# Softmax times V over 96 heads on one core: loads four heads ahead on SyncE, stores on the GpSimd queue, the cast of v on VectorE

## The chip, the cores and the metric

The kernel runs on one core of one Trainium2 chip. A core has a matrix engine (TensorE, in the profile PE, with its weight loads as PEld), VectorE (DVE), ScalarE (ACT), GpSimd (POOL) and SyncE (SP), which only waits and issues transfers here. All transfers between the device memory (HBM) and the on-chip buffer run on the core's 16 DMA engines. The metric is the device time of one launch in microseconds (us); lower is better. The time quoted is the median of several runs. A profile is of one single execution.

## The reference

Scores of 8 x 12 = 96 heads are given, 1024 x 1024 float32 for each head, and v, 1024 x 64 float32 for each head. The result is the softmax of the scores times v:

```python
batch, n_heads, seq, head_dim = 8, 12, 1024, 64
scores_max = np.max(scores, axis=-1, keepdims=True)
attn = np.exp(scores - scores_max)
attn = attn / (np.sum(attn, axis=-1, keepdims=True) + 1e-8)
return np.matmul(attn, v).astype(np.float32)
```

For each head 4 MB of scores and 256 KB of v come in, and 256 KB of result go out.

## The kernel before, in words

The loop runs over the 96 heads (`BH`), and in each head over `R` = 8 blocks of 128 query rows. One load brings the v of a head into `v_sb` (L100), and one load its scores into `s_nat` (L104): partition p holds query rows 8p to 8p+7, so each partition reads 32 KB that lie together. Only the last head loads its scores in four pieces of two blocks.

The work on a head goes through four engines. GpSimd casts v from float32 to fp16 into one of three buffers `vones` (L107), whose 65th column is a constant 1.0, so that the matrix product gives the row sums beside the result. ScalarE takes the exponential of two blocks at a time, `s_nat` to `p_nat` in fp16 (L113, four per head; no maximum is subtracted). TensorE transposes each block in eight 128 x 128 pieces into PSUM, `psT` (L117), VectorE copies them back, `pt` (L123), and TensorE multiplies them with `vones` into `psO`, eight matmuls that accumulate (L76). In the source the product of a block comes two blocks later than its transposes (`LAG` = 2, the list `pending` and the function `finish`). After each four blocks VectorE takes the reciprocal of the sums (L87) and multiplies (L88) into `out_sb`. When a head's eight blocks are done, one store writes `out_sb` back (L95).

Loads and stores are all issued by SyncE, one after the other: an instruction that has to wait there holds up every one behind it. SyncE issues the store of a head when VectorE has finished that head's `out_sb`. There are four buffers each for `s_nat` and `v_sb`, three for `out_sb`, six for `p_nat`, five for `pt`, five for `psT` and three for `psO`. A framework works out the semaphores and the order in which each engine gets its instructions; that order, and not only the order of the source lines, says which load stands behind which store.

Of the kernel before, what the change touches and what calls it, by code (L numbers as in the profile page):

```python
# [1 line left out]

# [5 lines left out]

FP32 = mybir.dt.float32
FP16 = mybir.dt.float16  # L10
EXP = mybir.ActivationFunctionType.Exp


@with_exitstack
def kernel(
    ctx: ExitStack,
    tc: tile.TileContext,
    scores: bass.AP,
    v: bass.AP,
    out: bass.AP,  # L20
):
    nc = tc.nc
    P = 128

    B, H, SQ, SK = scores.shape
    Bv, Hv, SKv, D = v.shape
    assert (B, H, SK) == (Bv, Hv, SKv)
    BH = B * H
    assert SQ % P == 0 and SK % P == 0
    R = SQ // P  # L30
    C = SK // P
    M = D + 1
    EB = 2
    G = 4
    LAG = 2
    NV = 3

    sc_bh = scores.rearrange("b h (p r) j -> (b h) p r j", p=P)  # L40
    v_bh = v.rearrange("b h (p c) d -> (b h) p c d", p=P)
    out_bh = out.rearrange("b h (p r) d -> (b h) p r d", p=P)

    const_pool = ctx.enter_context(tc.tile_pool(name="const", bufs=1))
    s_pool = ctx.enter_context(tc.tile_pool(name="spool", bufs=4))
    p_pool = ctx.enter_context(tc.tile_pool(name="ppool", bufs=6))
    v_pool = ctx.enter_context(tc.tile_pool(name="vpool", bufs=4))
    pt_pool = ctx.enter_context(tc.tile_pool(name="ptpool", bufs=5))
    ob_pool = ctx.enter_context(tc.tile_pool(name="obpool", bufs=3))
    rc_pool = ctx.enter_context(tc.tile_pool(name="rcpool", bufs=4))  # L50
    psT_pool = ctx.enter_context(tc.tile_pool(name="psTp", bufs=5, space=bass.MemoryType.PSUM))
    psO_pool = ctx.enter_context(tc.tile_pool(name="psOp", bufs=3, space=bass.MemoryType.PSUM))

    ident32 = const_pool.tile([P, P], FP32, name="ident32")
    make_identity(nc, ident32)
    ident16 = const_pool.tile([P, P], FP16, name="ident16")
    nc.vector.tensor_copy(out=ident16[:], in_=ident32[:])  # L57


    vones_bufs = []  # L60
    for k in range(NV):
        vo = const_pool.tile([P, C, M], FP16, name=f"vones{k}")
        nc.vector.memset(vo[:, :, D : D + 1], 1.0)  # L63
        vones_bufs.append(vo)

    pending = []

    def finish(u):

        n, r, pt, st = u  # L70
        g = r % G
        if g == 0:
            st["psO"] = psO_pool.tile([P, G, M], FP32, tag="psO", name="psO")
        psO = st["psO"]
        for c in range(C):
            nc.tensor.matmul(  # L76
                out=psO[:, g, :],
                lhsT=pt[:, c * P : (c + 1) * P],
                rhs=st["vones"][:, c, :],
                start=(c == 0),  # L80
                stop=(c == C - 1),
            )
        if g == G - 1:
            if r == G - 1:
                st["out_sb"] = ob_pool.tile([P, R, D], FP32, tag="out_sb", name="out_sb")
            recip = rc_pool.tile([P, G, 1], FP32, tag="recip", name="recip")
            nc.vector.reciprocal(out=recip[:], in_=psO[:, :, D : D + 1])  # L87
            nc.vector.tensor_tensor(  # L88
                out=st["out_sb"][:, r - G + 1 : r + 1, :],
                in0=psO[:, :, 0:D],  # L90
                in1=recip[:].to_broadcast([P, G, D]),
                op=mybir.AluOpType.mult,
            )
        if r == R - 1:
            nc.sync.dma_start(out=out_bh[n], in_=st["out_sb"][:])  # L95

    for n in range(BH):
        last = n == BH - 1
        v_sb = v_pool.tile([P, C, D], FP32, tag="v_sb", name="v_sb")
        nc.sync.dma_start(out=v_sb[:], in_=v_bh[n])  # L100
        s_nat = s_pool.tile([P, R, SK], FP32, tag="s_nat", name="s_nat")
        step = EB if last else R
        for r in range(0, R, step):
            nc.sync.dma_start(out=s_nat[:, r : r + step, :], in_=sc_bh[n, :, r : r + step, :])  # L104

        vones = vones_bufs[n % NV]
        nc.gpsimd.tensor_copy(out=vones[:, :, 0:D], in_=v_sb[:])  # L107
        st = dict(vones=vones)

        for r in range(R):  # L110
            if r % EB == 0:
                p_nat = p_pool.tile([P, EB, SK], FP16, tag="p_nat", name="p_nat")
                nc.scalar.activation(out=p_nat[:], in_=s_nat[:, r : r + EB, :], func=EXP)  # L113
            p_row = p_nat[:, r % EB, :].rearrange("p (q c) -> p c q", c=C)
            psT = psT_pool.tile([P, SK], FP16, tag="psT", name="psT")
            for c in range(C):
                nc.tensor.transpose(  # L117
                    out=psT[:, c * P : (c + 1) * P],
                    in_=p_row[:, c, :],
                    identity=ident16[:],  # L120
                )
            pt = pt_pool.tile([P, SK], FP16, tag="pt", name="pt")
            nc.vector.tensor_copy(out=pt[:], in_=psT[:])  # L123
            pending.append((n, r, pt, st))
            if len(pending) > LAG:
                finish(pending.pop(0))
    while pending:
        finish(pending.pop(0))


# [1 line left out]
_INS = ['scores', 'v']  # L132
_OUTS = [((8, 12, 1024, 64), 'float32')]


# [23 lines left out]
```

## Time and profile before

| What | Value |
|---|---|
| median of 3 runs | 1283.77 us (1282.96 to 1286.11) |
| the profiled execution | 1278.68 us, its span from first to last instruction 1276.9 us |
| PE, PEld busy | 797.7 us (62%), 760.6 us (60%) |
| ACT busy | 703.9 us (55%) |
| DVE busy | 619.7 us (49%) |
| POOL busy | 60.1 us (5%) |
| HBM read, written | 427.82 MB, 25.17 MB |
| mean granted TensorE clock | 0.764 of full speed |

Busy time is the time in which an engine executes something; issuing a transfer and waiting do not count. "L95" is line 95 of the kernel. In a list of groups, "<-" gives what was written and from what, then shapes, the count, the busy time, the mean duration of one in nanoseconds, and the time that the engine was idle just before, with what ended that idle time. The DMA lines give in tenths how busy the 16 DMA engines were in each of 40 equal slices, and the rate in each. The chain is the work that ended last, followed back from the end, each step to the thing that released it. SPq and POOLq are the instruction queues of SyncE and GpSimd.

### The profile page before, as it was taken

How to read it: one execution, taken by the hardware profiler on the slowest of the kernel's cores; microseconds unless marked ns; L12 is line 12 of the kernel's file. 1: busy time of each engine (PE TensorE's matmuls, PEld its weight loads, DVE VectorE, ACT ScalarE, POOL GpSimd, SP SyncE). 2: the span in 40 equal slices, each digit the busy share in tenths (PEclk: the TensorE clock that was granted, in tenths of full speed). 3: DMA queues.
4: the chain of work that ended last, by engine and by line, in shares of the span. 5: the costliest groups of instructions: out<-in, count | busy, mean ns of one | idle time of the engine just before them, and what ended most of it. 6: DMA issues, size and time to landing. Idle time of an engine off the chain costs nothing.

```text
span 1276.9 us, 27588 instructions
## 1 busy us (share of the span) xinstructions
PE 797.7 (62%) x12288; PEld 760.6 (60%) x12288; DVE 619.7 (49%) x1156; ACT 703.9 (55%) x385; POOL 60.1 (5%) x102
## 2 busy tenths in 40 slices
PE   4666576665656657566665656666575655656656
PEld 4566565665656556556655656656565655656556
DVE  3445454454555445445454544545454544545545
ACT  4464564655646455554645556465565645556465
POOL 0000000000000000000000000000000000000000
PEclk9777778777787777777777787778777777777778
DMA  9888988988979889898999889899888989879886
GB/s 402 327 358 365 356 363 347 377 351 358 377 316 368 365 358 378 329 370 348 360 377 365 362 345 375 334 364 377 361 363 328 366 363 376 362 312 374 356 346 264
DMA packets 42023, 454.76 MB, mean 356 GB/s; under 512 B 4656, under 2 KB 4656, under 8 KB 29232
## 3 DMA queue, kind: packets, MB, share of 16 engines
q1 hardware_dynamic: 41904, 453.00, 87.9%
q8 instruction: 96, 1.57, 0.5%
q14 instruction: 23, 0.19, 0.0%
HBM read 427.82 MB, written 25.17 MB: 355 GB/s over the span
## 4 chain that ended last, share of the span: by engine, by line
DMA 51%; PE 23%; DVE 8%; ACT 8%; issue 6%; SPq 4%; ACTq 0%
DMA s_nat<-in_scores_dram 51%; PE psT L117 17%; ACT p_nat L113 8%; PE psO L76 6%; DVE pt L123 4%; DVE out_sb L88 3%; SPq L100 2%; DVE recip L87 1%; SPq L95 1%; ACTq L113 0%; SPq L104 0%
## 5 line engine op out<-in xcount | busy, mean ns | idle before, releaser
L113 ACT ACTIVATE p_nat<-s_nat 128x2048 f16<-128x2048 f32 x384 | 702.6, 1900 | 564.7 <-DMA s_nat<-in_scores_dram 553.3
L117 PE MATMUL psT<-ident,p_nat 128*128 128x128 f16 x6144 | 634.9, 269 | 435.3 <-ACT p_nat L113 435.2
L123 DVE COPY pt<-psT 128x1024 f16<-128x1024 f16 x768 | 529.1, 690 | 599.5 <-PE psT L117 587.3
L117 PEld LDWEIGHTS <-p_nat 128*128 128x128 f16 x6144 | 538.5, 156 | 460.2 <-ACT p_nat L113 450.5
L76 PE MATMUL psO<-vones,pt 128*128 128x65 f16 x6144 | 345.6, 205 | 40.0 <-DVE pt L123 40.0
L76 PEld LDWEIGHTS <-pt 128*128 128x128 f16 x6144 | 298.4, 107 | 52.2 <-DVE pt L123 52.2
L107 POOL CAST vones<-v_sb 128x512 f16<-128x512 f32 x96 | 59.4, 619 | 1196.0 <-DMA v_sb<-in_v_dram 1094.1
L88 DVE TENSOR_TENSOR out_sb<-psO,recip 128x256 f32<-128x256 f32 x192 | 80.6, 420 | 3.3
L87 DVE RECIPROCAL recip<-psO 128x4 f32<-128x4 f32 x192 | 34.1, 178 | 50.0 <-PE psO L76 50.0
L113 ACT ACT_TABLE_LOAD x1 | 1.3, 1283 | 0.7 <-PEq L143 0.7
L63 DVE MEMSET vones<- 128x8 f16 x3 | 0.1, 65 | 0.8 <-PEq L143 0.8
L57 DVE CAST ident<-ident 128x128 f16<-128x128 f32 x1 | 0.2, 226 | 0.4 <-POOL ident masks.py:199 0.4
masks.py:199 POOL TENSOR_SCALAR_AFFINE_SELECT ident<-ident 128x128 f32<-128x128 f32 x1 | 0.3, 294 | 0.1
masks.py:197 POOL MEMSET ident<- 128x128 f32 x1 | 0.2, 205 | 0.3 <-POOLq L143 0.3
L143 POOL MEMSET const-float32-0.0<- 128x1 f32 x1 | 0.1, 99 | 0.2 <-issue 0.2
L143 POOL MEMSET const-bfloat16-1.0<- 128x1 bf16 x1 | 0.1, 102 | 0.0
L143 POOL MEMSET const-uint8-127<- 128x1 uint8 x1 | 0.1, 102 | 0.0
L143 POOL MEMSET const-float32-1.0<- 128x1 f32 x1 | 0.1, 99 | 0.0
## 6 DMA issues: line engine op xcount, KB each, us to landing
s_nat<-in_scores_dram SPq DMA_DIRECT2D x95, 4096.0 KB, 13.8
v_sb<-in_v_dram SPq DMA_DIRECT2D x96, 256.0 KB, 3.1
out_dram<-out_sb SPq DMA_DIRECT2D x96, 256.0 KB, 2.4
s_nat<-in_scores_dram SPq DMA_DIRECT2D x4, 1024.0 KB, 8.9
```

What stands on the lines that cost most here:

```text
L57: nc.vector.tensor_copy(out=ident16[:], in_=ident32[:])
L63: nc.vector.memset(vo[:, :, D : D + 1], 1.0)
L76: nc.tensor.matmul(out=psO[:, g, :], lhsT=pt[:, c * P : (c + 1) * P], rhs=st["vones"][:, c, :], start=(c == 0), stop=(c == C - 1),)
L87: nc.vector.reciprocal(out=recip[:], in_=psO[:, :, D : D + 1])
L88: nc.vector.tensor_tensor(out=st["out_sb"][:, r - G + 1 : r + 1, :], in0=psO[:, :, 0:D], in1=recip[:].to_broadcast([P, G, D]), op=mybir.Al ...
L95: nc.sync.dma_start(out=out_bh[n], in_=st["out_sb"][:])
L100: nc.sync.dma_start(out=v_sb[:], in_=v_bh[n])
L107: nc.gpsimd.tensor_copy(out=vones[:, :, 0:D], in_=v_sb[:])
L113: nc.scalar.activation(out=p_nat[:], in_=s_nat[:, r : r + EB, :], func=EXP)
L117: nc.tensor.transpose(out=psT[:, c * P : (c + 1) * P], in_=p_row[:, c, :], identity=ident16[:],)
L123: nc.vector.tensor_copy(out=pt[:], in_=psT[:])
L143: nc = _bacc.Bacc("TRN2", target_bir_lowering=False, num_devices=1)
```

## The change

Four things change. The loads are issued by a function `load`: four heads (`AHEAD` = 4) ahead of the loop, and then the load of head n + 4 at the last block of head n, after that head's exponentials. Each load is made to follow the load before it in SyncE's queue (`queue`, an order without a semaphore). The stores go out on GpSimd's queue. The cast of v is done by VectorE. The buffers stay as many as before (`AHEAD` is 4, as the counts were).

```diff
+    AHEAD = 4
...
-    s_pool = ctx.enter_context(tc.tile_pool(name="spool", bufs=4))
+    s_pool = ctx.enter_context(tc.tile_pool(name="spool", bufs=AHEAD))
...
-    v_pool = ctx.enter_context(tc.tile_pool(name="vpool", bufs=4))
+    v_pool = ctx.enter_context(tc.tile_pool(name="vpool", bufs=AHEAD))
...
         if r == R - 1:
-            nc.sync.dma_start(out=out_bh[n], in_=st["out_sb"][:])
+            nc.gpsimd.dma_start(out=out_bh[n], in_=st["out_sb"][:])
+
+    queued = []
+
+    def queue(dma):
+
+        if queued:
+            tc.add_manual_dep(
+                dma.ins,
+                queued[-1].ins.name,
+                mybir.DependencyInfo(mybir.DependencyClass.NoSync, mybir.DependencyReason.DATA),
+                reason="queue order",
+            )
+        queued.append(dma)
+
+    loaded = {}
+
+    def load(n):
+        v_sb = v_pool.tile([P, C, D], FP32, tag="v_sb", name="v_sb")
+        queue(nc.sync.dma_start(out=v_sb[:], in_=v_bh[n]))
+        s_nat = s_pool.tile([P, R, SK], FP32, tag="s_nat", name="s_nat")
+        step = EB if n == BH - 1 else R
+        for r in range(0, R, step):
+            queue(
+                nc.sync.dma_start(out=s_nat[:, r : r + step, :], in_=sc_bh[n, :, r : r + step, :])
+            )
+        loaded[n] = (s_nat, v_sb)
+
+    for n in range(min(AHEAD, BH)):
+        load(n)

     for n in range(BH):
-        last = n == BH - 1
-        v_sb = v_pool.tile([P, C, D], FP32, tag="v_sb", name="v_sb")
-        nc.sync.dma_start(out=v_sb[:], in_=v_bh[n])
-        s_nat = s_pool.tile([P, R, SK], FP32, tag="s_nat", name="s_nat")
-        step = EB if last else R
-        for r in range(0, R, step):
-            nc.sync.dma_start(out=s_nat[:, r : r + step, :], in_=sc_bh[n, :, r : r + step, :])
-
+        s_nat, v_sb = loaded.pop(n)
         vones = vones_bufs[n % NV]
-        nc.gpsimd.tensor_copy(out=vones[:, :, 0:D], in_=v_sb[:])
+        nc.vector.tensor_copy(out=vones[:, :, 0:D], in_=v_sb[:])
...
             nc.vector.tensor_copy(out=pt[:], in_=psT[:])
+            if r == R - 1 and n + AHEAD < BH:
+                load(n + AHEAD)
             pending.append((n, r, pt, st))
```

SyncE at the start of the program, before. The names carry numbers that count up with the heads: `s_nat_97`, `_252`, `_427`, `_602`, `_777` are the scores of heads 0 to 4, and `out_sb_205`, `_380`, `_555` the results of heads 0, 1 and 2.

```order
L100 DMA v_sb_95<-in_v_dram 128x512
L104 DMA s_nat_97<-in_scores_dram 128x8192
L100 DMA v_sb_250<-in_v_dram 128x512
L104 DMA s_nat_252<-in_scores_dram 128x8192
L100 DMA v_sb_425<-in_v_dram 128x512
L104 DMA s_nat_427<-in_scores_dram 128x8192
L95 DMA out_0_dram<-out_sb_205 128x512
L95 DMA out_0_dram<-out_sb_380 128x512
L100 DMA v_sb_600<-in_v_dram 128x512
L104 DMA s_nat_602<-in_scores_dram 128x8192
L95 DMA out_0_dram<-out_sb_555 128x512
L100 DMA v_sb_775<-in_v_dram 128x512
```

From then on the load of head n + 2 stands behind the store of head n. The same place on SyncE in the changed kernel (`s_nat_97`, `_101`, `_105`, `_109`, `_256`, `_431` are heads 0 to 5), with the semaphores on which a row waits:

```order
L115 DMA v_sb_95<-in_v_dram 128x512
L120 DMA s_nat_97<-in_scores_dram 128x8192
L115 DMA v_sb_99<-in_v_dram 128x512
L120 DMA s_nat_101<-in_scores_dram 128x8192
L115 DMA v_sb_103<-in_v_dram 128x512
L120 DMA s_nat_105<-in_scores_dram 128x8192
L115 DMA v_sb_107<-in_v_dram 128x512
L120 DMA s_nat_109<-in_scores_dram 128x8192
L115 DMA v_sb_254<-in_v_dram 128x512 [waits DMAHW0_49,DVE_49]
L120 DMA s_nat_256<-in_scores_dram 128x8192 [waits DMAHW1_49,Activation_49]
L115 DMA v_sb_429<-in_v_dram 128x512 [waits DMAHW2_49,DVE_49]
L120 DMA s_nat_431<-in_scores_dram 128x8192 [waits DMAHW3_49,Activation_49]
```

The stores have left SyncE, four heads are loaded before anything waits, and from head 4 on the load of v waits for the cast four heads earlier (on VectorE) and the load of the scores for the exponentials four heads earlier (on ScalarE).

VectorE around the change from head 0 to head 1, before (`out_sb_205` is head 0's result, `pt_266` and `pt_285` the first two blocks of head 1):

```order
L123 COPY pt_240<-psT_231 128x1024
L87 RECIPROCAL recip_295<-psO_222 128x4
L88 TENSOR_TENSOR out_sb_205<-psO_222,recip_295 128x256
L123 COPY pt_266<-psT_257 128x1024
L123 COPY pt_285<-psT_276 128x1024
```

And in the changed kernel (`out_sb_217` is head 0's result, `pt_278` and `pt_297` the first two blocks of head 1, `vones2_93<-v_sb_103` the cast of head 2's v):

```order
L146 COPY pt_252<-psT_243 128x1024
L88 RECIPROCAL recip_307<-psO_234 128x4
L89 TENSOR_TENSOR out_sb_217<-psO_234,recip_307 128x256
L130 CAST vones2_93<-v_sb_103 128x8x64
L146 COPY pt_278<-psT_269 128x1024
L146 COPY pt_297<-psT_288 128x1024
```

Between the last multiplication of a head and the first copy of the next there is now one cast, and it is the cast for the head after that one: the copies of head 1 stand behind the cast of head 2's v, those of head 2 behind the cast of head 3's, and so on. GpSimd is left with the 96 stores, each of which waits for VectorE, and from the ninth on for the landing of the store eight before it.

## The prediction

> **What bounds the kernel now.** First the page: how long, and which engine is full.
>
> ```profile
> span 1276.9 us, 27588 instructions
> PE 797.7 (62%) x12288; PEld 760.6 (60%) x12288; DVE 619.7 (49%) x1156; ACT 703.9 (55%) x385; POOL 60.1 (5%) x102
> ...
> DMA packets 42023, 454.76 MB, mean 356 GB/s; under 512 B 4656, under 2 KB 4656, under 8 KB 29232
> ...
> q1 hardware_dynamic: 41904, 453.00, 87.9%
> q8 instruction: 96, 1.57, 0.5%
> ```
>
> No compute engine is busy for two thirds of the span. The DMA engines are at 87.9 + 0.5 = 88.4%, so they are near their limit but not at it: 11.6%, or 148 us, they stand still. The chain and the waits say why.
>
> ```profile
> DMA s_nat<-in_scores_dram 51%; PE psT L117 17%; ACT p_nat L113 8%; PE psO L76 6%; DVE pt L123 4%; DVE out_sb L88 3%; SPq L100 2%; DVE recip L87 1%; SPq L95 1%; ACTq L113 0%; SPq L104 0%
> ```
> ```profile
> SPq L95 <- DVE out_sb L88: 1110.7, 96, 21.5
> ```
> ```profile
> ACT p_nat L113 <- DMA s_nat<-in_scores_dram: 553.3, 92, 11.6
> ```
>
> The chain alternates: half of it is the load of scores, the rest the head's way through ACT, PE and DVE, and back to SyncE. SyncE waits 1110.7 us at the stores (L95) for VectorE, and the next load stands behind each store. ACT in turn waits 553.3 us for loads. The timeline of SyncE shows one turn of the circle:
>
> ```profile
> 605.40 0.34 SPq L95 DMA_DIRECT2D out_dram<-out_sb  x1
> 605.84 0.38 SPq L100 DMA_DIRECT2D v_sb<-in_v_dram  x1
> 606.31 0.40 SPq L104 DMA_DIRECT2D s_nat<-in_scores_dram  x1
> 616.61 0.34 SPq L95 DMA_DIRECT2D out_dram<-out_sb  x1
> 617.04 1.07 SPq L100 DMA_DIRECT2D v_sb<-in_v_dram  x1
> 618.21 0.38 SPq L104 DMA_DIRECT2D s_nat<-in_scores_dram  x1
> 632.03 0.34 SPq L95 DMA_DIRECT2D out_dram<-out_sb  x1
> 632.47 0.38 SPq L100 DMA_DIRECT2D v_sb<-in_v_dram  x1
> 632.94 0.41 SPq L104 DMA_DIRECT2D s_nat<-in_scores_dram  x1
> ```
>
> The scores issued at 606.31 come back as a store at 632.03, and the load of the head after next leaves at 632.94: 26.63 us for two heads, 13.3 each, and 96 x 13.3 = 1278, the span. So the bound is a circle of load and compute with two heads in it, closed by SyncE's order. The windows show what it costs the DMA engines (columns: stretch, its length, busy time of each engine, granted clock, DMA share, GB/s):
>
> ```profile
> core 0: us, PE busy (x) PEld busy (x) DVE busy (x) ACT busy (x) POOL busy (x), PEclk, DMA share, GB/s
> 13.60:24.00 10.40, 8.04 (x122) 7.80 (x123) 5.86 (x10) 7.32 (x5) 0.62 (x1) 1.00 1.02 436
> 606.30:618.20 11.90, 7.86 (x128) 7.49 (x128) 6.46 (x12) 6.69 (x4) 0.62 (x1) 0.82 1.00 400
> 618.20:632.90 14.70, 8.86 (x128) 8.49 (x128) 6.46 (x12) 9.02 (x5) 0.62 (x1) 0.68 0.79 321
> ```
>
> Fed without a gap they move 400 to 436 GB/s; where the next load is late, 321.
>
> **The change, part by part.** *Stores leave SyncE and the loads run four heads ahead.* This opens the circle. The load of head n + 4 now waits for ACT's last exponential of head n, 7.32 us after that head has landed (the window's four), and there are then the heads n + 1 to n + 3 still queued. The queue should never run dry, and the DMA engines set the pace. Their price is the bytes, 454.76 MB, over the rate of a full queue, and for that I have rows from both sides:
>
> ```profile
> DMA packets 574, 8.88 MB, mean 423 GB/s; under 512 B 62, under 2 KB 62, under 8 KB 319
> ...
> q1 hardware_dynamic: 574, 8.88, 99.0%
> ```
>
> This is the stretch from 3 to 24 us, where three heads were queued at once: loads alone, 423 GB/s, 1075 us for all bytes. The best stretch (436) gives 1043 us; 606.3 to 618.2, with stores and v among the scores and a share of 1.00, gives 1137 at 400 GB/s; the packets of today laid end to end, 88.4% of the span, give 1129. I take the middle of 423 and 400, 411.5 GB/s: **1105 us**, since the new stream has stores in it, as the second row has, but no starts from an empty queue, as the first. Ahead of it lies the start, 2.0 us:
>
> ```profile
> 0.00:2.00 2.00, 0.00 (x0) 0.00 (x0) 0.36 (x4) 1.27 (x1) 0.70 (x6) 1.00 0.19 13
> 2.00:4.00 2.00, 0.00 (x0) 0.00 (x0) 0.00 (x0) 0.01 (x1) 0.40 (x1) 1.00 1.07 380
> ```
>
> Behind it lies the way of the last two blocks, priced from groups and from the chain in order of time:
>
> ```profile
> 620.08 1.92 ACT p_nat L113
> ...
> 625.36 0.85 PE psT L117 x8
> 626.21 0.44 PE psO L76 x8
> ```
> ```profile
> L123 DVE COPY pt<-psT 128x1024 f16<-128x1024 f16 x768 | 529.1, 690 | 599.5 <-PE psT L117 587.3
> ...
> L107 POOL CAST vones<-v_sb 128x512 f16<-128x512 f32 x96 | 59.4, 619 | 1196.0 <-DMA v_sb<-in_v_dram 1094.1
> L88 DVE TENSOR_TENSOR out_sb<-psO,recip 128x256 f32<-128x256 f32 x192 | 80.6, 420 | 3.3
> L87 DVE RECIPROCAL recip<-psO 128x4 f32<-128x4 f32 x192 | 34.1, 178 | 50.0 <-PE psO L76 50.0
> ...
> L57 DVE CAST ident<-ident 128x128 f16<-128x128 f32 x1 | 0.2, 226 | 0.4 <-POOL ident masks.py:199 0.4
> ...
> out_dram<-out_sb SPq DMA_DIRECT2D x96, 256.0 KB, 2.4
> ```
>
> An exponential 1.92, two blocks on PE 2 x 1.29, a copy 0.69, a last product 0.44, reciprocal and multiply 0.60, the store to landing 2.4: 8.6 us, and I say 9 with the issue. The sum is 2 + 1105 + 9 = 1116 us of span.
>
> *What is late next.* A head would then come every 11.5 us. ACT needs 7.32 of it. DVE has 6.46 and one cast more. PE in the slow rows above (clock 0.68 in that window) takes 0.85 + 0.44 = 1.29 us a block, 10.3 a head, and less when the clock is up (8.04 busy at 1.00 in 13.6 to 24). All stay under 11.5, PE by the least.
>
> *The cast goes from GpSimd to VectorE.* GpSimd's is 59.4 us in all (L107 above), idle 1196.0 us before it, so nothing is gained by its going. On VectorE the trace has no cast of 128x512 float32; the same operation on a quarter of it takes 226 ns (L57), the copy of twice the elements 690 (L123). I take 0.5 us, between 0.23 and 0.9 (four times 226); 48 us in all, to 668 busy. VectorE's idle time hides it, 587.3 us before the copies alone; without that cover it would cost its 48. As the order shows, the cast for head n + 1 stands ahead of the copies of head n, so all copies of head n, PE's products and the p_nat buffers behind them wait until v of head n + 1 is there. It is queued right behind the scores of head n, 256 KB, 0.6 us at 423 GB/s, while the first copy of head n needs an exponential (1.92) and eight transposes first. As long as the queue is full the wait is covered, and I cost it at nothing.
>
> *The store on GpSimd.* Its issue cost there is not in the trace. The nearest rows are SyncE's own issues (shortest, median and longest in ns):
>
> ```profile
> L100 SPq DMA_DIRECT2D v_sb<-in_v_dram x96: 327/384/1556, 0.7 to 1251.7; - x96
> ```
>
> They take 0.33 to 1.56 us, and GpSimd has nothing else left to do, so I take nothing. A store may be late by two heads (three `out_sb` buffers) before VectorE's multiply waits for it. That the store shares the DMA engines from another queue is the open point, next.
>
> **The rivals.** *A: a switch between queues costs.* In the old kernel loads and stores are on one queue, q1. What a foreign packet costs there is seen in q8: 96 packets of 16.4 KB hold 0.5% of 16 x 1276.9 us, 1.06 us each, where q1's 39.6 ns a KB (87.9% for 453.00 MB) would give 0.65. A foreign packet is thus some 0.4 us dearer, 0.3 to 0.5 by the rounding. A store has 8 packets on each of 16 engines (29232 - 4656 = 24576 of 2 KB, over 192 transfers of v and result). If each of them cost 0.41 more, a head would take 3.3 us more and the kernel 1116 + 315 = 1431 us: slower. One such cost per store gives +39, 1155; three, +118, 1234. It decides from four per store on: (1277 - 1116) / 96 = 1.7 us a head. Against it: q8's packets come from another source, singly, and the engines may hold both queues ready. By the Trainium skill ("DMA: Bandwidth & Descriptors", Queues, rings and completion order) a DMA engine takes the queues in turn and empties a whole packet of some 9 to 17 descriptors before it goes to the next; by that rule a store would be one switch and the sum 1155. No row here shows how a store is cut.
>
> *B: the long-run rate is capped.* The middle of the run moves 356 GB/s on the whole page, and the longest stretch above 400 that I have is the first 32 us (402 in the first slice):
>
> ```profile
> GB/s 402 327 358 365 356 363 347 377 351 358 377 316 368 365 358 378 329 370 348 360 377 365 362 345 375 334 364 377 361 363 328 366 363 376 362 312 374 356 346 264
> ```
>
> If memory gave no more than the 356 to 358 of the middle over a long time, the span would be 454.76 MB / 357 = 1274 + 11 = 1285, no change. Against it: a share of 0.79 stands beside the 321, and 400 comes with 1.00, at 606 us as at 13; the low mean goes with idle engines. By the Trainium skill (the same page, Specifications) the memory's limit for a core is about 358 GB/s, which would be this case; the 423 and 436 above speak against it for one core alone.
>
> *C: the change does not do what it says.* A load could still wait for the late part of the circle. By the order it waits for ACT and the cast only; then ACT would end up with the old 553.3 us of waits and the time at 1278.
>
> **How the numbers follow.** The profiled execution is 1278.68 us, 1.8 above its span, and the median 1283.77 is 1.004 of it. (1116 + 1.8) x 1.004 = **1122 us**. Chances: forecast, from 436 to 400 GB/s, 1060 to 1155: 0.64. A mild (two or three switch costs, 1155 to 1240): 0.17. A hard (slower, 1285 to 1435): 0.12. B: 0.05, C: 0.02, both about no change. The range takes in forecast and mild A, and leaves out the hard A, B and C; the low end is cut to 1070, 432 GB/s, since stores are in the stream: 1070 to 1240. Faster by over 0.3%, about what a measurement of this kernel can tell from no change: 0.64 + 0.17 = 0.81; within it 0.06 (B, C, less a part); slower 0.13.
>
> **What would show it.** Right: DMA share 97% or more in every slice, 400 to 425 GB/s, the chain nearly all loads of scores, SyncE's waits on ACT instead of DVE, ACT waiting about 4 us a head, and VectorE's casts near 0.5 us with no wait of length. The store of a head may land late, 10 us and more. Wrong: a share near 100% with a rate under 380 GB/s is A or B; A if packets of the scores got longer where stores run beside them, B if they are longer all the time. Gaps in the DMA row mean C, or that copies wait behind a cast. PE waiting for nothing means compute became the bound.

## The result, and the profile after

The changed kernel takes 1094.79 us (median of 4 runs, 1094.51 to 1095.15) against 1283.69 us before. The ratio is 0.8526, with a 95% interval of 0.8511 to 0.8541: 14.7% less time. 1122 us was forecast, 1070 to 1240 the range. The profiled execution took 1095.15 us, its span 1093.4 us.

The page of the changed kernel, in the parts that were shown of before:

```profile
span 1093.4 us, 27493 instructions
...
PE 784.1 (72%) x12288; PEld 745.6 (68%) x12288; DVE 656.1 (60%) x1252; ACT 704.0 (64%) x385; POOL 55.4 (5%) x102
...
DMA  9999999999999999999999999999999999999982
GB/s 394 428 430 426 429 427 425 424 426 431 425 432 423 423 429 426 426 429 428 429 421 430 425 424 433 422 432 425 424 427 421 435 423 424 428 425 428 428 363 93
...
q1 hardware_dynamic: 28080, 427.83, 92.0%
q0 software_dynamic: 7680, 25.17, 5.7%
q8 instruction: 96, 1.57, 0.6%
...
L96 POOL DMA_DIRECT2D out_dram<-out_sb x96 | 54.7, 570 | 1028.7 <-DVE out_sb L89 1028.7
...
L130 DVE CAST vones<-v_sb 128x512 f16<-128x512 f32 x96 | 41.1, 428 | 47.1 <-DMA v_sb<-in_v_dram 46.4
...
s_nat<-in_scores_dram SPq DMA_DIRECT2D x95, 4096.0 KB, 36.8
v_sb<-in_v_dram SPq DMA_DIRECT2D x96, 256.0 KB, 37.3
out_dram<-out_sb POOLq DMA_DIRECT2D x96, 256.0 KB, 10.7
```

The DMA row is full from the first slice to the last but two, and no slice in between is under 421 GB/s. The busy time of TensorE and ScalarE is nearly what it was; they do the same work in a shorter span. VectorE has the casts in addition, and what GpSimd has left is the issue of the stores. q0 is GpSimd's queue, and holds the stores. A load now takes 37 us from issue to landing, since three others stand before it.

SyncE's waits in the changed kernel, longest first (us in total, times, longest):

```profile
SPq L120 <- ACT p_nat L136: 680.7, 92, 7.4
SPq L120 <- DMA s_nat<-in_scores_dram: 276.8, 93, 8.4
SPq L179 <- DMA out_dram<-out_sb: 42.8, 2, 37.5
SPq L115 <- DVE pt L146: 14.4, 41, 0.5
SPq L179 <- PEq L179: 6.2, 2, 5.7
```

The 1110.7 us at the stores are gone. SyncE now waits for ScalarE, or for the older load whose semaphore it uses again, and with a full queue neither costs anything. What the span holds besides the full stream is at its end. The windows of the changed kernel, the middle first, then 3 us each:

```profile
4.00:1040.00 1036.00, 750.16 (x11728) 713.46 (x11729) 625.81 (x1191) 673.58 (x368) 51.91 (x91) 0.81 1.01 427
```
```profile
1052.00:1055.00 3.00, 1.07 (x26) 0.82 (x23) 2.04 (x6) 1.09 (x1) 0.54 (x1) 1.00 1.00 416
1055.00:1058.00 3.00, 2.12 (x19) 2.00 (x20) 0.85 (x2) 3.00 (x3) 0.01 (x1) 0.63 0.76 314
...
1067.00:1070.00 3.00, 3.00 (x33) 2.87 (x33) 1.61 (x3) 3.00 (x2) 0.00 (x0) 0.50 0.53 220
1070.00:1073.00 3.00, 3.00 (x42) 3.00 (x40) 1.79 (x3) 3.00 (x3) 0.00 (x0) 0.52 0.51 213
1073.00:1076.00 3.00, 3.00 (x65) 3.00 (x64) 2.67 (x7) 3.00 (x3) 0.00 (x0) 1.00 0.30 120
1076.00:1079.00 3.00, 3.00 (x65) 3.00 (x64) 2.91 (x7) 3.00 (x2) 0.37 (x1) 1.00 0.00 0
...
1088.00:1091.00 3.00, 0.00 (x0) 0.00 (x0) 0.00 (x0) 0.00 (x0) 0.00 (x0) 0.50 0.00 0
```

All 16 DMA engines are busy to 1055 us. Then the share falls, to 0.76 in the next 3 us and to a half by 1070, and the last scores land near 1075: by then only about eight engines are still bringing in scores. From 1088 us nothing is busy at all, and the span still runs for 5 us.

### The profile page after: what moved, and what is told of

It reads as the page before. It is cut to its first block, busy times and chain, and to the rows that moved or that the text cites. A ratio compares the mean times of both kernels' runs of the same rounds, so it can differ in the third digit from the quotient of the medians.

```text
span 1093.4 us, 27493 instructions
## 1 busy us (share of the span) xinstructions
PE 784.1 (72%) x12288; PEld 745.6 (68%) x12288; DVE 656.1 (60%) x1252; ACT 704.0 (64%) x385; POOL 55.4 (5%) x102
## 2 busy tenths in 40 slices
DMA packets 35879, 454.76 MB, mean 416 GB/s; under 512 B 4656, under 2 KB 4656, under 8 KB 23088
## 3 DMA queue, kind: packets, MB, share of 16 engines
q1 hardware_dynamic: 28080, 427.83, 92.0%
q0 software_dynamic: 7680, 25.17, 5.7%
HBM read 427.82 MB, written 25.17 MB: 414 GB/s over the span
## 4 chain that ended last, share of the span: by engine, by line
issue 87%; POOL 5%; DMA 5%; PE 1%; ACT 1%; DVE 0%; POOLq 0%; SPq 0%; ACTq 0%
POOL out_dram L96 5%; DMA s_nat<-in_scores_dram 5%; ACT p_nat L136 1%; PE psT L140 1%; PE psO L77 0%; DVE pt L146 0%; DVE out_sb L89 0%; POOLq L96 0%; DVE recip L88 0%; POOLq L179 0%; SPq L115 0%; ACTq L136 0%
## 5 line engine op out<-in xcount | busy, mean ns | idle before, releaser
L140 PE MATMUL psT<-ident,p_nat 128*128 128x128 f16 x6144 | 621.6, 263 | 259.0 <-ACT p_nat L136 258.6
L140 PEld LDWEIGHTS <-p_nat 128*128 128x128 f16 x6144 | 525.3, 155 | 285.4 <-ACT p_nat L136 279.1
L96 POOL DMA_DIRECT2D out_dram<-out_sb x96 | 54.7, 570 | 1028.7 <-DVE out_sb L89 1028.7
L130 DVE CAST vones<-v_sb 128x512 f16<-128x512 f32 x96 | 41.1, 428 | 47.1 <-DMA v_sb<-in_v_dram 46.4
## 6 DMA issues: line engine op xcount, KB each, us to landing
out_dram<-out_sb POOLq DMA_DIRECT2D x96, 256.0 KB, 10.7
```

Of the source, the lines that this page charges most:

```text
L96: nc.gpsimd.dma_start(out=out_bh[n], in_=st["out_sb"][:])
L130: nc.vector.tensor_copy(out=vones[:, :, 0:D], in_=v_sb[:])
L140: nc.tensor.transpose(out=psT[:, c * P : (c + 1) * P], in_=p_row[:, c, :], identity=ident16[:],)
```

## The experiments

**One part alone.** The gain could be due to the stores leaving SyncE, to the written order of the loads, or to the cast. The first kernel is the old one with one line changed:

```diff
-            nc.sync.dma_start(out=out_bh[n], in_=st["out_sb"][:])
+            nc.gpsimd.dma_start(out=out_bh[n], in_=st["out_sb"][:])
```

> The kernel before with one line changed: the store on GpSimd's queue; loads in the loop, the cast of v on GpSimd. Theory T (the gain is the store leaving SyncE, since only the store's wait for VectorE held the loads; the framework then orders the same loads four heads ahead by itself): 1090 to 1105 us, DMA share near 1, SyncE waiting for ACT and no longer for VectorE. Rival R1 (the written order of loads ahead is what keeps the queue full): above 1150 us. Rival R2 (the cast has to leave GpSimd, since stores and casts now wait behind one another there): 1150 to 1280 us, with TensorE or VectorE waiting for the cast.

Measured: 1094.8 us, ratio 0.8529 (0.8511 to 0.8546). SyncE's waits in this kernel (L104 is the load of scores, L113 the exponential):

```profile
SPq L104 <- ACT p_nat L113: 680.9, 92, 7.4
SPq L104 <- DMA s_nat<-in_scores_dram: 276.8, 93, 8.5
```

That is the whole gain, with the same waits as in the changed kernel. SyncE's order at its start is now, without a word on it in the source (numbers as before, heads 0, 3 and 4):

```
1 L100 DMA v_sb_95<-in_v_dram 128x512
2 L104 DMA s_nat_97<-in_scores_dram 128x8192
...
7 L100 DMA v_sb_600<-in_v_dram 128x512
8 L104 DMA s_nat_602<-in_scores_dram 128x8192
9 L100 DMA v_sb_775<-in_v_dram 128x512 [waits DMAHW0_49,Pool_49]
10 L104 DMA s_nat_777<-in_scores_dram 128x8192 [waits DMAHW1_49,Activation_49]
```

Four heads go ahead, then each load of scores waits for ScalarE (and each load of v for the cast, here on GpSimd): with no store between them, the four buffers alone give the order that the function `load` writes out. The next kernel adds the cast on VectorE to this one:

```diff
-        nc.gpsimd.tensor_copy(out=vones[:, :, 0:D], in_=v_sb[:])
+        nc.vector.tensor_copy(out=vones[:, :, 0:D], in_=v_sb[:])
```

> As e1, and the cast on VectorE; only the function that loads ahead is missing of the change. Theory T: the same as the changed kernel, 1093 to 1097 us. R1: above 1150 us. R2: as the changed kernel, and e1 clearly slower than this.

Measured: 1094.8 us, 0.8528 (0.8511 to 0.8546). The cast's place makes no difference beside the store, nor the function that loads ahead beside both. Alone in the old kernel, with the same edit:

> The kernel before with only the cast of v moved to VectorE. Theory T: no change within 0.5%, 1277 to 1290 us, since nobody waited for the cast on GpSimd and VectorE is idle half the time. R2: several per cent, either way.

Measured: 1284.87 us, 1.0015 (0.9994 to 1.0036): no change. R2 falls with e1, and R1 with e1 and e2.

**The stores back on SyncE, but behind the loads.** If the store's wait was harmful only by standing ahead of loads that could have been issued, it may stay on SyncE once enough loads go before it:

```diff
-            nc.gpsimd.dma_start(out=out_bh[n], in_=st["out_sb"][:])
+            nc.sync.dma_start(out=out_bh[n], in_=st["out_sb"][:])
```

> The changed kernel with its stores back on SyncE: the load of head n+4 now stands ahead of the store of head n. Theory T: SyncE's wait for a store no longer starves the queue, because three heads are queued ahead of it; but a store lands only behind those loads, some 30 to 45 us after its issue, and VectorE may wait for an out_sb buffer. 1088 to 1120 us. Rival R3 (any store on the loads' queue holds the loads, whatever the order): 1250 us and more.

Measured: 1090.02 us, 0.8491 (0.847 to 0.8512). From its page, and its waits:

```profile
q1 hardware_dynamic: 41904, 453.00, 98.5%
...
out_dram<-out_sb SPq DMA_DIRECT2D x96, 256.0 KB, 32.3
```
```profile
DVE out_sb L89 <- DMA out_dram<-out_sb: 92.6, 91, 2.9
```

R3 falls. A store now lands 32.3 us after its issue, behind three heads of scores, and VectorE waits 92.6 us for free `out_sb` buffers, which costs nothing beside a full queue. So there are two ways to the same gain: take the stores out of the loads' queue (e1, without loads ahead), or send the loads ahead of them (this kernel). Each suffices.

**Why the engines end unevenly.** The eight late engines could be those that bring in TensorE's instructions: q8 has 96 packets of 16.4 KB, one for each head. The kernel for this leaves out part of the computation: TensorE transposes and multiplies only the first half of the key pieces, and VectorE copies half, so that half of TensorE's instructions go.

```diff
-        for c in range(C):
+        for c in range(C // 2):
             nc.tensor.matmul(
...
-            for c in range(C):
+            for c in range(C // 2):
                 nc.tensor.transpose(
...
-            nc.vector.tensor_copy(out=pt[:], in_=psT[:])
+            nc.vector.tensor_copy(out=pt[:, : SK // 2], in_=psT[:, : SK // 2])
```

> The changed kernel with TensorE working on the first half of the key pieces only (4 of 8 transposes and products in each block; the copy takes half as well); loads, stores, exponentials and casts are as in the changed kernel. TensorE has 12288 instructions instead of 24576, so 48 packets of q8 instead of 96. Theory F (the DMA engines end unevenly, half of them some 17 us after the others, because those also bring in TensorE's instructions, at about 1.45 us for each packet): the stretch at the end in which only part of the engines works shrinks to half, the last load lands near 1066 us instead of 1075, span 1078 to 1084. Rival M (half of the engines are slower for another reason, a memory port or the stores): that stretch stays at some 17 to 20 us and the last load lands near 1073 to 1076.

Measured: 1084.45 us (one run), span 1082.6. Its q8 row, its windows, and the last exponentials:

```profile
q8 instruction: 48, 0.79, 0.3%
```
```profile
1055.00:1060.00 5.00, 2.09 (x19) 1.66 (x20) 1.28 (x3) 4.17 (x3) 0.54 (x1) 0.50 0.82 338
1060.00:1065.00 5.00, 4.63 (x48) 3.52 (x46) 2.97 (x8) 5.00 (x4) 0.00 (x0) 0.50 0.58 241
1065.00:1070.00 5.00, 4.51 (x47) 3.51 (x45) 3.25 (x10) 5.00 (x3) 0.54 (x1) 0.50 0.22 82
```
```profile
1055.83 14.52 ACT L136 ACTIVATE p_nat<-s_nat 128x2048 f16<-128x2048 f32 x8 [3.68 <-DMA s_nat<-in_scores_dram]
```

And the same exponentials in the changed kernel:

```profile
1064.89 14.53 ACT L136 ACTIVATE p_nat<-s_nat 128x2048 f16<-128x2048 f32 x8 [3.66 <-DMA s_nat<-in_scores_dram]
```

The stretch in which only part of the engines works is shorter by half (some 10 us instead of 20), and head 94, with which these exponentials begin, lands 9.06 us earlier. Over eight engines 48 packets are 6 each, so one costs its engine 1.5 us. That is theory F in number and shape.

No view names the DMA engine of a packet, but the trace's packet records settle it. In a full queue a packet begins within a few ns of the end of the one before it on its engine, so the records can be laid end to end into 16 chains, apart from a few places where two chains cannot be told apart. In the changed kernel, up to the end of the full stretch, the packets of q8 then lie on eight of the chains, one packet a head, these eight in turn. At the 94th head these eight chains are 18 to 20 us behind, 1.6 us for each of their 11 or 12 packets, and five of the others are level to within 1 us. (The last three, which have nearly all of q14's few packets of instructions, are 4 to 12 us behind.) In the kernel with half the keys eight chains again take turns, five or six packets each, and are 8 to 10 us behind. The stores are no reason for the uneven end: in e3, where they are on q1, the share also stays between 0.5 and 0.7 from 1060 to 1075. What the kernel with half the keys cannot tell apart is whether the half of VectorE's and TensorE's work that went with it also helped a little; the rate in the middle is 428 GB/s against 427.

**How far ahead.** In the changed kernel:

```diff
-    AHEAD = 4
+    AHEAD = 2
```

> The changed kernel with AHEAD = 2, so two buffers for scores and v. Theory D (depth serves two ends: a queue that never runs dry, for which two heads are nearly enough, since the load of head n+2 leaves some 3.7 us before head n+1 has landed; and room for the DMA engines to run apart, which two heads do not give, so that each head waits for its slowest engine): 1130 to 1220 us, DMA share 0.88 to 0.97. Rival S (depth beyond two is worth nothing): 1093 to 1100 us.

Measured: 1103.78 us (one run). Neither: D was far too high, S somewhat low. With three:

> The changed kernel with AHEAD = 3. Two ahead gave 1103.78 us, between the two theories: dearer than the changed kernel by 9 us, but far less than theory D asked. If the 9 us are the price of a queue that the fast engines find empty at times, three ahead removes them: 1094 to 1097 us, and the rate in the middle of the run is 427 GB/s again (two ahead: 420). If every head of depth less costs the same: 1098 to 1101 us.

Measured: 1094.49 us (one run). The middle of the run, with two ahead, then with three:

```profile
4.00:1030.00 1026.00, 739.89 (x11520) 703.86 (x11520) 616.49 (x1172) 660.48 (x361) 50.88 (x90) 0.81 1.01 420
```
```profile
4.00:1030.00 1026.00, 744.71 (x11634) 708.31 (x11635) 620.69 (x1182) 666.22 (x364) 51.48 (x90) 0.81 1.01 426
```

Three heads are as good as four; two cost 9 us, spread over the run. D's mistake was to charge each head for its slowest engine anew. The late engines take turns bringing in instructions, as the chains above show, so that one that was late for one head is not the late one for the next; that this is what keeps the price low is argued, not shown. The 7 GB/s that two heads ahead lose at a share of 1.01 are in the length of the packets: in the records a 32 KB packet of scores takes 1.24 us in the mean with two heads ahead, 1.22 with four.

**The end.** The last store lands 2.3 us after its issue, which begins at 1084.15 us, and the span ends at 1093.4. In the list of SyncE's waits above the last 5.7 us are a wait of the closing (L179). Only the last store is moved:

```diff
-            nc.gpsimd.dma_start(out=out_bh[n], in_=st["out_sb"][:])
+            eng = nc.sync if n == BH - 1 else nc.gpsimd
+            eng.dma_start(out=out_bh[n], in_=st["out_sb"][:])
```

> The changed kernel with only the last head's store on SyncE. In the changed kernel the last store lands some 3 us after its issue, and the span ends 6 us later. Theory G (GpSimd needs these 6 us to close its store queue after the last landing, and with the last store elsewhere it does so while the last head is computed): 1088 to 1090 us. Rival (the end is as long on any queue, or GpSimd's closing starts only when all engines are done): 1094 to 1096 us.

Measured: 1089.2 us, 0.8478 (0.8459 to 0.8497), and the wait of the closing is 1.0 us:

```profile
SPq L180 <- PEq L180: 1.5, 2, 1.0
```

The time is as theory G has it: a last store from GpSimd costs 5.6 us at the end. The wait at the closing says the same: its longest is 5.7 us in every kernel here whose last store GpSimd issues, and 0.4 to 1.0 us where SyncE does. That the time goes into closing GpSimd's queue is not shown; the profile puts the wait down to TensorE's sequencer (PEq). It fits that e3, which has no store on GpSimd, is at 1090.02. The last kernel adds pieces for the last head but one:

```diff
-        step = EB if n == BH - 1 else R
+        step = EB if n >= BH - 2 else R
```

> As e7, and the scores of the last two heads in four pieces each, not of the last alone. In the changed kernel ScalarE starts head 94 only when all of it has landed (1064.9 us), and then works through the two heads without a stop to 1079.4, 4 us after the last load landed. If that is what sets the end: 1084 to 1087 us. If the pieces of the last two heads land too close together, or wait for one another at issue: as e7, 1088 to 1091 us.

Measured: 1086.57 us, 0.8457 (0.8438 to 0.8476), the fastest of all. ScalarE's timeline at the end:

```profile
1054.02 16.41 ACT L137 ACTIVATE p_nat<-s_nat 128x2048 f16<-128x2048 f32 x9 [3.81 <-DMA s_nat<-in_scores_dram]
1071.01 1.92 ACT L137 ACTIVATE p_nat<-s_nat 128x2048 f16<-128x2048 f32 x1 [0.58 <-DMA s_nat<-in_scores_dram]
1074.09 1.91 ACT L137 ACTIVATE p_nat<-s_nat 128x2048 f16<-128x2048 f32 x1 [1.17 <-DMA s_nat<-in_scores_dram]
1076.59 1.92 ACT L137 ACTIVATE p_nat<-s_nat 128x2048 f16<-128x2048 f32 x1 [0.59 <-PE psO L77]
```

ScalarE now starts on head 94 piece by piece, waits for pieces of head 95 and ends at 1078.5 instead of 1079.4; the loads set the end again, and with them the uneven engines.

## Why the prediction was right, point by point

**The bound.** Right, and shown: the circle of two heads was closed by the store's wait ahead of the loads. Moving that one line gives all of the gain (e1). The prediction took the loads' new order and the stores' new queue as one step; e1 and e3 show that each alone is enough.

**The rate.** The term of the stream was sized too high. 411.5 GB/s was taken as the middle of 423 and 400, and 427 were measured over 1036 us: 454.76 / 427 = 1065 us where 1105 stood, 40 less. The row at 400 GB/s had a share of 1.00, but packets that were longer, since each load there started from an empty queue: over the whole old run q1 needed 39.6 ns a KB, in the changed kernel 92.0% of 16 x 1093.4 us for 427.83 MB, 37.6. The packet records of the old run show where: of the eight packets of scores that each engine has in a load, the first takes 1.56 us in the mean, the others 1.21 to 1.25; in the changed kernel the mean of all is 1.22. The row at 423, with three heads queued, was the one that resembled the new state, but for the stores, and those cost hardly more than other bytes (see rival A).

**The end.** Sized too low: 2 us of start and 1065 of stream leave 26.4 us of the span for the way out, where 9 stood. The last store on GpSimd is 5.6 of it (e7). The rest is that the engines are not done together, so that scores still come in at 1075, and that ScalarE can start on head 94 only at 1064.89 and then has two heads of work, 14.5 us; e8 takes 2.6 us off that. The two errors go against each other, -40 and +17. With the factor 1.004 of the old run, which the new one does not have, the forecast was off by 27 us, 2.4%; that it came so near is in part luck.

**The cast.** 428 ns each, 0.5 us was taken, 41 us in all and hidden, as e2 against e1 and e4 show. VectorE waits 46.4 us for v ahead of it, more than "no wait of length" said, but it costs nothing.

**The store on GpSimd.** Its issue takes 0.57 us, within the bounds, and it lands after 10.7 us in the middle of the loads, as forecast.

**Rival A**'s price did not come about. A KB in q0 costs 5.7% of 16 x 1093.4 us for 25.17 MB, 39.6 ns, and with the stores in q1 (e3) all of q1 costs 37.9; loads beside stores from another queue run at the same 427 GB/s as behind stores in their own (426 in e3 from 4 to 1030 us). The 0.4 us of extra cost read from q8 was real, but it belongs to fetching instructions: it is 1.5 us a packet with what follows (e5), and does not carry over to stores. In the chains of packet records a store is four packets of 4 KB on each engine, which as a rule stand singly between two packets of a load, with no more time between packets of two queues than between packets of one. So a store did bring the four switches from which on A was to decide; it is their price that is nothing. The rule of the Trainium skill ("DMA: Bandwidth & Descriptors", Queues, rings and completion order) that an engine takes the queues in turn by whole packets agrees with these records, if a packet is what the profile calls one; whether it holds 9 to 17 descriptors no record here says.

**Rival B** did not come about: 427 GB/s held over the run. The limit of about 358 GB/s in the Trainium skill (the same page, Specifications) does not bind this core when it runs alone. **Rival C** did not either; SyncE waits for ScalarE, as the order said.

**The signs.** A full DMA row, SyncE's waits on ScalarE, a late store and the length of the cast came as named, and ScalarE's wait of some 4 us a head:

```profile
ACT p_nat L136 <- DMA s_nat<-in_scores_dram: 363.9, 92, 11.4
```

Two did not. The slices lie at 421 to 435 GB/s, more than half of them above the 425 that was named. And the chain of the changed kernel is not nearly all loads of scores; with the last store on SyncE (e7, the second line) it is, for the most part:

```profile
issue 87%; POOL 5%; DMA 5%; PE 1%; ACT 1%; DVE 0%; POOLq 0%; SPq 0%; ACTq 0%
```
```profile
DMA 78%; ACT 12%; issue 5%; PE 4%; DVE 1%; ACTq 0%; SPq 0%
```

The chain is followed back from the last work, which is GpSimd's store, and from there it goes along the issues of GpSimd. So it is no evidence here, for the loads or against them; the DMA row and the windows are.

## What to carry to other kernels

An instruction that waits late in the work must not stand in one queue ahead of loads that could go at once; look for it in the waits of the issuing engine, not in the busy shares. To size a stream that is to be kept full, take the rate from a stretch of the trace in which several loads were queued, here the first 24 us, and not from one that is busy but starts each load anew. When the loads bound the time, the next thing is the end: the last loads in pieces, and the last store from SyncE.

## What the runs showed that was not expected

The DMA engines also bring in TensorE's instructions, 16.4 KB for each head here, and eight of the 16 engines do that, in turn. Each packet costs its engine 1.5 to 1.6 us, and with a full queue these engines ended some 20 us after the first to be done; half the instructions took 9 us off. A last store from GpSimd costs 5.6 us at the end that one from SyncE does not. And a queue of stores beside a full queue of loads cost nothing measurable, neither in rate nor in time, though each store took 10.7 us to land instead of 2.4.
